# Two-layer diffusion trunk on one core: state tables, weight cuts and the context tail in another order

## The chip, the core and the metric

The kernel runs on one core of a Trainium2 chip. The metric is device time in microseconds (us), the median of several executions; lower is better. In what follows PE or TensorE is the matrix engine, DVE is VectorE, ACT is ScalarE, POOL is GpSimd, and SP is the engine that issues the DMAs named here. TensorE runs at one of two clock levels, 1.2 or 2.4 GHz; the profile gives the granted clock as a share of the higher one.

## The reference, cut to what matters

A latent stream `h` (1024 tokens by 1024) and a context stream `hc` (256 tokens) pass through two layers. Every layer is a mixer and a SwiGLU feed-forward, each behind a modulated RMSNorm and a gate. The context stream ends with layer 0's feed-forward; layer 1 uses its norm alone.

```python
for layer in range(2):
    sh1, sc1, g1, sh2, sc2, g2 = adaln(c, mod_w[layer], mod_b[layer])
    csh1, csc1, cg1, csh2, csc2, cg2 = adaln(c_ctx, mod_w[layer], mod_b[layer])
    n_lat = rms_norm(h, norm_g[layer, 0]) * (1 + sc1) + sh1
    n_ctx = rms_norm(hc, norm_g[layer, 0]) * (1 + csc1) + csh1
    if layer == 0:   # FNet groups + windowed attention, one input and one output projection
        o_lat, o_ctx = fourier_attention_mix(n_lat, n_ctx, mix_w_in, mix_w_out, ...)
    else:            # bidirectional diagonal state-space layer + GLU, context as its prefix
        o_lat, _ = s5_mix(n_lat, n_ctx, a_re, a_im, log_dt, b, c, d, glu_w)
    h = h + g1 * o_lat
    h = h + g2 * swiglu(rms_norm(h, norm_g[layer, 1]) * (1 + sc2) + sh2, w_gate, w_up, w_down)
    if layer == 0:
        hc = hc + cg1 * o_ctx
        hc = hc + cg2 * swiglu(rms_norm(hc, norm_g[layer, 1]) * (1 + csc2) + csh2, w_gate, w_up, w_down)
return rms_norm(h, final_g)
```

The state-space layer needs tables that depend on its parameters alone: for each pair of its 64 groups (32 "channels" here) a drive table, a readout table and a short kernel.

## The kernel before, in words

Each f32 matmul is three: both operands are split into a high half (a cast on ScalarE, `...h`) and a low half (a subtraction on VectorE, `...l`), and `mm3` (L155 to L157) multiplies high by high, low by high and high by low. A "cut" is the making of the two halves of a weight block (L1219, L1220); in layer 0's feed-forward the blocks of a weight pair are called A11, A12, A21 and A22, and S1 to S4 are sums of them, since the feed-forward on the latent rows goes by a Strassen scheme of seven products for eight.

The stretches on the time axis that the change touches:

- 175 to 300 us: the QKV projection, a loop over column blocks m in the order 4, 5, 0, 1, 2, 3, over three groups of tokens and over eight k steps (L942 to L970). The generator `tables(0, 12)` is stepped inside this loop, at k 2 and 5, and makes the tables of channels 0 to 11.
- 602 to 826: the context feed-forward, a loop over 22 units of 128 hidden columns (L1695 to L1733). Unit u cuts the weights of unit u+1 (`ccut`), runs its gate and up product (`cgate`, operand of the context `cx`), the down product of unit u-1 (`cdowns`) and the activation (`chidden`). In the middle of the gate `side()` steps `tables(12, 20)` and `prepare()`, which norms the latent rows for what follows.
- 826 to 845: the context tail (L1735 to L1753): gate, residual, sum of squares, norm, and eight stores to `udram`, from where the state-space layer reads the context.
- 826 to 1270: the steps `FA.step(s)` of the latent feed-forward, s from 0 to 10, with products pX, pY and pZ.
- 1270 to 1527: `FA.down`, the down projection on combined weights in raw slots (`rr`), with `tick0` once in 24 matmuls. It steps `behind2`, which holds `tables(20, 32, apart=True)` and `ssm_toeplitz` (whose last DMAs write `mtab`), and adds the residual of finished token tiles.
- 1527 to 1728: the state-space layer's front: `eload` brings drive tables (`El`) from DRAM, `pec` multiplies them with the context, ScalarE keeps the result (L1853), and the scan follows.

A table goes through `table_load` (its parameters by DMA, L576), `table_drive` (four copies on ScalarE, L584, and six products on GpSimd, L587 to L589, for one channel), `table_turn` (four transposes on TensorE, L596, a copy on ScalarE, L598, and a store to `etab`), `table_read` (four small matmuls, L608, a copy on ScalarE, L614, six products on VectorE, L619 to L621, and a store to `ftab`) and, for each second channel, `ssm_kt` (L628). The generator yields between these steps, and one call of it (`run(t, 1)`) goes as far as the next yield.

What sets the order: from the context feed-forward to the start of the scan SP, DVE, ACT and POOL issue in the order in which the code is written, one instruction behind the other, and an instruction that waits holds up all behind it on its engine. In the QKV loop only TensorE keeps the written order; a scheduler orders the others. `ctile()` gives one of six buffers in turn, raw slots (`wr0`, `wr1`, ...) are placed by name, and both are free again when their last reader is done.

## Time and profile before

| | us |
|---|---|
| median of 3 executions | 2667.91 (2664.15 to 2668.31) |
| profiled execution, device time | 2667.99 |
| profiled execution, span | 2666.2 |
| TensorE busy in the span | 2446.9 |
| VectorE busy | 1719.2 |
| ScalarE busy | 998.2 |
| GpSimd busy | 616.2 |

The mean granted clock of TensorE is 0.966. The span runs from the first to the last instruction of the profiled execution, and all positions on the time axis are counted from its start. A table of busy time tells which engine is loaded; where TensorE stands still is read from its list of waits, which names the line that waited, the engine and line that released it, and how long. From there the way leads to the releasing engine's timeline.

### The profile page before, as it was taken

How to read it: one execution, taken by the hardware profiler on the slowest of the kernel's cores; microseconds unless marked ns; L12 is line 12 of the kernel's file. 1: busy time of each engine (PE TensorE's matmuls, PEld its weight loads, DVE VectorE, ACT ScalarE, POOL GpSimd, SP SyncE). 2: the span in 40 equal slices, each digit the busy share in tenths (PEclk: the TensorE clock that was granted, in tenths of full speed). 3: DMA queues.
4: the chain of work that ended last, by engine and by line, in shares of the span. 5: the costliest groups of instructions: out<-in, count | busy, mean ns of one | idle time of the engine just before them, and what ended most of it. 6: DMA issues, size and time to landing. Idle time of an engine off the chain costs nothing.

```text
span 2666.2 us, 33521 instructions
## 1 busy us (share of the span) xinstructions
PE 2446.9 (92%) x12396; PEld 1967.4 (74%) x12396; DVE 1719.2 (64%) x2925; ACT 998.2 (37%) x1656; POOL 616.2 (23%) x867
## 2 busy tenths in 40 slices
PE   7999999997998999999899876499998999999996
PEld 4777677876897788888677654198876788887785
DVE  3648677675657766676577659932247676665556
ACT  4233466224554222222344482341253222223333
POOL 1235310122300122112444157511111112211000
PEclk9999999998999999999999987899999999999998
DMA  7642445535573544445766755624123545447653
GB/s 254 181 150 77 170 142 151 171 108 175 189 245 89 174 152 159 161 141 175 265 211 202 227 167 189 214 73 141 40 87 111 182 137 174 151 154 256 214 189 119
DMA packets 306900, 437.65 MB, mean 164 GB/s; under 512 B 71472, under 2 KB 176736, under 8 KB 306352
## 3 DMA queue, kind: packets, MB, share of 16 engines
q1 hardware_dynamic: 303600, 425.74, 48.0%
q0 software_dynamic: 3136, 9.77, 1.1%
q8 instruction: 98, 1.61, 0.2%
q14 instruction: 66, 0.54, 0.1%
HBM read 329.39 MB, written 111.17 MB: 165 GB/s over the span
## 4 chain that ended last, share of the span: by engine, by line
PE 65%; DVE 15%; ACT 5%; DMA 3%; issue 2%; SPq 0%; POOL 0%; DVEq 0%; ACTq 0%
PE pY L155 4%; PE pY L157 4%; PE pY L156 4%; PE pd L156 3%; PE pd L155 3%; PE pd L157 3%; PE pZ L157 3%; PE pZ L155 3%; PE pZ L156 3%; PE pX L157 3%; PE pX L155 3%; DVE SA L1990 3%; PE pX L156 3%; PE pft L2089 2%; PE pgl L155 2%
## 5 line engine op out<-in xcount | busy, mean ns | idle before, releaser
L1404 DVE TENSOR_TENSOR dl<-rr,dh 128x1024 fp32r<-128x1024 f32 x156 | 190.6, 1265 | 153.6 <-ACT dh L1403 153.6
L156 PE MATMUL pd<-dl,dh 128*128 128x512 f32 x616 | 244.6, 397 | 11.1 <-DVE dl L1404 11.1
L155 PE MATMUL pd<-dh 128*128 128x512 f32 x616 | 246.0, 399 | 7.2 <-DVE du L1425 2.4
L157 PE MATMUL pd<-dh,dl 128*128 128x512 f32 x616 | 242.9, 394 | 0.0
L1403 ACT CAST dh<-rr 128x1024 fp32r<-128x1024 f32 x156 | 153.8, 1034 | 194.5 <-PE pd L156 188.9
L1271 POOL TENSOR_TENSOR wd<-wd 128x512 f32<-128x512 f32 x22 | 32.2, 1464 | 810.6 <-DMA wd<-in_ffn_w_down 810.6
L1240 ACT ACTIVATE c<-c 128x512 f32<-128x512 f32 x66 | 41.8, 633 | 405.5 <-DVE c L1320 218.5
L156 PEld LDWEIGHTS pd<-dl,dh 128*128 128x128 f32 x616 | 117.4, 191 | 39.6 <-DVE dl L1404 16.0
L155 PEld LDWEIGHTS pd<-dh 128*128 128x128 f32 x616 | 117.4, 191 | 36.9 <-DVE du L1425 3.2
L157 PEld LDWEIGHTS pd<-dh,dl 128*128 128x128 f32 x616 | 117.3, 190 | 24.7
L155 PE MATMUL pgl<-wl_h,yTh 128*128 128x512 f32 x256 | 100.7, 393 | 0.0
L156 PE MATMUL pgl<-wl_l,yTh 128*128 128x512 f32 x256 | 100.1, 391 | 0.0
L1209 DVE TENSOR_TENSOR wr<-wr 128x1024 f32<-128x1024 f32 x65 | 99.1, 1525 | 1.4
L1990 DVE TENSOR_TENSOR SA<-SA,scan 128x48 f32<-128x48 f32 x508 | 91.1, 238 | 0.0
L2180 DVE TENSOR_TENSOR gsg<-gsg,pgl 128x256 f32<-128x256 f32 x32 | 13.4, 420 | 106.2 <-ACT gsg L2179 106.2
L1241 DVE TENSOR_TENSOR c<-c 128x512 f32<-128x512 f32 x66 | 47.6, 721 | 46.2 <-ACT c L1240 46.2
L227 PE MATMUL ada<-mw,cond 128*32 128x512 f32 x320 | 58.7, 622 | 18.8 <-DMA mw<-in_mod_w 18.7
L155 PE MATMUL pY<-xT2h,S2h 128*128 128x512 f32 x176 | 70.7, 402 | 4.7 <-ACT S2h L1219 4.7
L1990 POOL TENSOR_TENSOR SB<-SB,scan 128x32 f32<-128x32 f32 x254 | 69.7, 274 | 20.8 <-ACT SB L1914 1.0
L1240 ACT ACTIVATE c<-pX 128x512 f32<-128x512 f32 x21 | 12.6, 601 | 161.6 <-PE pX L157 161.6
L157 PE MATMUL pY<-xT2h,S2l 128*128 128x512 f32 x176 | 70.5, 400 | 2.6 <-DVE S2l L1220 2.6
L155 PE MATMUL pY<-xT3h,S3h 128*128 128x512 f32 x176 | 69.7, 396 | 3.1 <-DVE c L1298 3.1
(761 smaller groups left out, 7342.2 us busy)
## 6 DMA issues: line engine op xcount, KB each, us to landing
mw<-in_mod_w SPq DMA_DIRECT2D x96, 512.0 KB
rr<-hd SPq DMA_DIRECT2D x70, 512.0 KB
wr<-in_ffn_w_gate SPq DMA_DIRECT2D x66, 512.0 KB
wr<-in_ffn_w_up SPq DMA_DIRECT2D x66, 512.0 KB
hd<-c SPq DMA_DIRECT2D x66, 512.0 KB
wd<-in_ffn_w_down SPq DMA_DIRECT2D x22, 1024.0 KB
td<-wd SPq DMA_DIRECT2D x88, 256.0 KB
rr<-td SPq DMA_DIRECT2D x40, 512.0 KB
```

The lines of the kernel that those rows point to most:

```text
L155: nc.tensor.matmul(o, ah, bh, start=first, stop=False, **kw)
L156: nc.tensor.matmul(o, ah, bl, start=False, stop=False, **kw)
L157: return nc.tensor.matmul(o, al, bh, start=False, stop=last, **kw)
L227: nc.tensor.matmul(acc[32 * t:32 * t + 32, :], cond[:, k, :], w[:, q * 512:(q + 1) * 512], start=(k == 0 and not act), stop=(k == 7), tile ...
L1209: eng.tensor_sub(b(n), b(x), b(y))
L1240: nc.scalar.activation(c[:, 0], src[:, 0], AF.Silu)
L1241: nc.vector.tensor_mul(c[:, 1], c[:, 0], src[:, 1])
L1271: e.tensor_sub(b11, b12, b11)
L1403: nc.scalar.copy(hi[:, 0:m], t[:, a, 0:m])
L1404: nc.vector.tensor_sub(lo[:, 0:m], t[:, a, 0:m], hi[:, 0:m].bitcast(F32))
L1990: eng.tensor_add(cur, cur, tm[:, b])
L2089: nc.tensor.matmul(o_, T_[:, :, c_, g0], F_[:, g, c_, :], start=(n_ >= 2 and c_ == 0), stop=(c_ == 1 and (n_ >= 2 or g == 3)))
```

## The change

1. `tables()` yields between a table's load and its drive, and makes its further empty turn in each case but the `apart` one, where before it made it only with `slots`. The QKV loop calls the generator twice ahead of the loop and, in column block 3, at k 1, 4 and 6.
2. In the context feed-forward units 0 and 1 are both cut ahead of the loop, and the loop's first turn cuts nothing.
3. The context tail is taken apart: the gating stays, into two buffers `sc`; adds, squares and norm with the stores become hooks that step 0 of the latent feed-forward calls behind its first cuts, behind its A12 product, and ahead of its S1 cut. The stores write 16 values (64 bytes) in a run where they wrote 32 (128 bytes).
4. At the end of the down projection `eput(1)` loads the second pair of drive tables into the raw slot `wr0` as soon as a single raw block is left; `eload` follows for the third and fourth pair, and later ones move up in the same way. The `mtab` DMAs go out two in a turn.

```diff
@@ tables
         table_load(a // 2)
+        yield
         table_drive(a)
         yield
-        if slots:
+        if not apart:
             yield
@@ ssm_toeplitz
             nc.sync.dma_start(mtab[16 * jj:16 * jj + 16], ...)
-            yield
+            if jj % 2:
+                yield
@@ QKV
-    run(tq, 1)
+    run(tq, 2)
...
-                if k in (2, 5) and (m, gi) != (4, 0):
+                if k in ((1, 4, 6) if m == 3 else (2, 5)) and (m, gi) != (4, 0):
                     run(tq, 1)
@@ FA
+        def hook(self, n):
+            self.hooks.pop(n, lambda: None)()
@@ FA.step
                 self.cut(s, "A12")
                 if s == 0:
                     self.cutx("T3")
+            self.hook("T3")
...
                 self.cut(s, "S3")
                 self.close_step(s)
+                self.hook("A12")
                 self.first_hidden(s)
+                self.hook("c11")
             c11 = self.c.pop(s)[1]
             self.cut(s, "S1")
@@ context feed-forward
     ccut(0, 0)
     ccut(0, 1)
+    ccut(1, 0)
+    ccut(1, 1)
     cload(1)
...
-        if u + 1 < NHT:
+        if u + 1 >= NHT:
+            FA.cut(0, "A11")
+        elif u:
             ccut(u + 1, 0)
-        else:
-            FA.cut(0, "A11")
...
-        if u + 1 < NHT:
+        if u + 1 >= NHT:
+            wops[u] = wsplit1(cwd.pop(u))
+        elif u:
             ccut(u + 1, 1)
-        else:
-            wops[u] = wsplit1(cwd.pop(u))
@@ context tail
-    g2c = FA.ctile().rearrange("p a n -> p (a n)")
-    nc.sync.dma_start(g2c, row(0, 5, 1))
-    hc = [FA.ctile().rearrange("p a n -> p (a n)") for _ in range(2)]
+    hc, sc = ([FA.ctile().rearrange("p a n -> p (a n)") for _ in range(2)] for _ in range(2))
+    nc.sync.dma_start(sc[1], row(0, 5, 1))
     for t in range(2):
         nc.sync.dma_start(hc[t], hdram[8 + t])
     FA.load(1)
     cdowns(NHT - 1, wops.pop(NHT - 1))
     for t in range(2):
-        sc = wp.tile([P, D], F32, name="cgt", tag="ws", bufs=2)
-        nc.vector.tensor_mul(sc, cacc[t].rearrange("p a n -> p (a n)"), g2c)
-        nc.vector.tensor_add(hc[t], hc[t], sc)
-        nc.scalar.activation(sc, hc[t], AF.Square, accum_out=ssF[:, 10 + t:11 + t])
+        nc.vector.tensor_mul(sc[t], cacc[t].rearrange("p a n -> p (a n)"), sc[1])
+    def ctx_add():
+        for t in range(2):
+            nc.vector.tensor_add(sc[t], sc[t], hc[t])
+    def ctx_square():
+        for t in range(2):
+            nc.scalar.activation(hc[t], sc[t], AF.Square, accum_out=ssF[:, 10 + t:11 + t])
     def ctx_store():
         rs = rstd_finish(ssF[:, 10:12], "rC")
-        for q in range(2):
-            uc = FA.ctile()...
-            for i in range(2):
-                nc.vector.tensor_scalar_mul(uc[:, :, i, :], hc[i][:, 512 * q:512 * q + 512]..., rs[:, i:i + 1])
+        for t in range(2):
+            nc.scalar.mul(sc[t], sc[t], rs[:, t:t + 1])
             for a in range(4):
-                nc.sync.dma_start(udram[:, 32 * q:32 * q + 32, a, :], uc[a::4]...)
-    ctx_store()
+                nc.sync.dma_start(udram[:, :, a, 16 * t:16 * t + 16], sc[t][a::4].rearrange("p (g h) -> p g h", h=16))
+    FA.hooks = {"T3": ctx_add, "A12": ctx_square, "c11": ctx_store}
@@ down projection
+    def eput(n_, slots):
+        for ch, t in zip((2 * order8[n_], 2 * order8[n_] + 1), slots):
+            Et[ch] = t.rearrange("p (a b n) -> p a b n", a=4, b=2)
+            nc.sync.dma_start(Et[ch]..., etab[2 * ch:2 * ch + 2]...)
     def tick0():
         flush()
+        if not FA.queue and len(FA.rawq) == 1:
+            t = FA.place("wr0", "El", [P, 4, 512]).rearrange("p a n -> p (a n)")
+            eput(1, (t[:, 0:1024], t[:, 1024:2048]))
...
     FA.down(gained0, tick0)
-    run(bt)
     run(bh)
     flush()
     h = hf_
-    for n_ in range(1, 3):
+    for n_ in range(2, 4):
         eload(n_)
+    run(bt)
...
-        if n_ + 3 < 8:
+        if n_ < 2:
+            eload(n_ + 4)
+        elif 3 <= n_ < 5:
             eload(n_ + 3)
```

ScalarE at the start of the context feed-forward, before. A11h to A22h are the high halves of a unit's weight cuts, L584 is the drive of table 12, and `csg` and `chid` are a unit's activation.

```order
L1219 CAST A11h<-wr 128x1024
L1219 CAST A12h<-wr 128x1024
L1219 CAST A21h<-wr 128x1024
L1496 ACTIVATE nFscr,ssF_4929<-hb 128x1024
L584 COPY tE<-tpar 64x2x16 x4
L282 ACTIVATE nFrs<-nFrs 128x8
L1219 CAST A22h<-wr 128x1024
L1634 ACT_TABLE_LOAD
L1634 ACTIVATE csg<-gu 128x256
L1637 CAST chid<-csg 128x256
L137 CAST cw_h<-c 128x1024
L1219 CAST A11h<-wr 128x1024
```

ScalarE at the same place, after.

```order
L1224 CAST A11h<-wr 128x1024
L1224 CAST A12h<-wr 128x1024
L1224 CAST A21h<-wr 128x1024
L1224 CAST A22h<-wr 128x1024
L1504 ACTIVATE nFscr,ssF_4929<-hb 128x1024
L282 ACTIVATE nFrs<-nFrs 128x8
L1642 ACT_TABLE_LOAD
L1642 ACTIVATE csg<-gu 128x256
L1645 CAST chid<-csg 128x256
L137 CAST cw_h<-c 128x1024
L1224 CAST A11h<-wr 128x1024
L584 COPY tE<-tpar 64x2x16 x4
```

Both cuts of unit 1 now stand ahead of the table's copies, and these stand between the two cuts of unit 2.

ScalarE at the context tail, before. The rows from S2h on belong to step 0; L1739 is the square, L282 the root of the context's norm, and `xT3h`, `xT1h` are operands of the latent rows.

```order
L1219 CAST S2h<-wr 128x1024
L1739 ACTIVATE cgt,ssF_4929<-c 128x1024 x2
L282 ACT_TABLE_LOAD
L282 ACTIVATE rCrs<-rCrs 128x2
L1247 COPY c<-pX 128x1024
L1219 CAST A12h<-wr 128x1024
L1186 CAST xT3h<-rawB 128x1024 x2
L1219 CAST S3h<-wr 128x1024
L1240 ACT_TABLE_LOAD
L1240 ACTIVATE c<-pX 128x512
L1219 CAST S1h<-ws_7961 128x1024
L1186 CAST xT1h<-rawB 128x1024 x2
```

ScalarE at the same place, after. L1755 is the square, L1760 the scaling by the norm.

```order
L1224 CAST S2h<-wr 128x1024
L1252 COPY c<-pX 128x1024
L1224 CAST A12h<-wr 128x1024
L1191 CAST xT3h<-rawB 128x1024 x2
L1224 CAST S3h<-wr 128x1024
L1755 ACTIVATE c,ssF_4929<-c 128x1024 x2
L1245 ACTIVATE c<-pX 128x512
L282 ACT_TABLE_LOAD
L282 ACTIVATE rCrs<-rCrs 128x2
L1760 ACTIVATE c<-c,rCrs 128x1024 x2
L1224 CAST S1h<-ws_7961 128x1024
L1191 CAST xT1h<-rawB 128x1024 x2
```

The first cuts of step 0 follow S2h at once, and square, root and scaling stand between the cuts of S3 and S1.

SP's DMAs at the end of the down projection, before. `El` are drive tables, `hdram` takes the residual rows.

```order
L683 DMA mtab<-rdram 1024x1x128
L1806 DMA hdram<-hf 128x1024
L683 DMA mtab<-rdram 1024x1x128
L1806 DMA hdram<-hf 128x1024 x2
L683 DMA mtab<-rdram 1024x1x128
L1806 DMA hdram<-hf 128x1024 x4
L683 DMA mtab<-rdram 1024x1x128 x3
L1565 DMA El<-etab 128x2x512 x14
```

SP at the same place, after.

```order
L1399 DMA rr<-in_ffn_w_down 128x512
L684 DMA mtab<-rdram 1024x1x128 x2
L1826 DMA hdram<-hf 128x1024
L684 DMA mtab<-rdram 1024x1x128 x2
L1826 DMA hdram<-hf 128x1024 x2
L1799 DMA El<-etab 128x2x512 x2
L1826 DMA hdram<-hf 128x1024 x4
L1573 DMA El<-etab 128x2x512 x12
```

One pair of drive tables stands ahead of the last four residual stores, and no `mtab` DMA is left behind them.

## Rows read from the trace of the kernel before

**Rows 1.** the page, part 1: busy us, share of the span, instructions

```profile
PE 2446.9 (92%) x12396; PEld 1967.4 (74%) x12396; DVE 1719.2 (64%) x2925; ACT 998.2 (37%) x1656; POOL 616.2 (23%) x867
```

**Rows 2.** TensorE's waits, QKV projection, 180 to 300: total, times, longest us

```profile
PE pet L596 <- POOL tab L589: 4.5, 2, 2.7
PE psw L817 <- DVE ql L152: 3.6, 3, 2.9
```

**Rows 3.** TensorE's waits at the start of the context feed-forward, 600 to 640

```profile
PE gu L155 <- ACT A22h L1219: 12.6, 1, 12.6
PE gu L157 <- DVE A22l L1220: 4.4, 1, 4.4
```

**Rows 4.** timeline, TensorE, context tail: start, duration, operation [idle before <- releaser]

```profile
844.82 0.79 PE L155 MATMUL pX<-xB21h,A12h 128*128 128x512 f32 x1 [5.39 <-ACT A12h L1219]
...
853.05 0.40 PE L155 MATMUL pY<-xT3h,S3h 128*128 128x512 f32 x1
853.28 0.39 PE L156 MATMUL pY<-xT3l,S3h 128*128 128x512 f32 x1
...
859.44 0.50 PE L155 MATMUL pZ<-xT1h,S1h 128*128 128x512 f32 x1 [0.62 <-ACT xT1h L1186]
```

**Rows 5.** TensorE's waits at the start of the down projection, 1265 to 1300

```profile
PE pet L596 <- POOL tE L589: 9.3, 2, 6.2
```

**Rows 6.** timeline, TensorE, start of the state-space layer

```profile
1545.88 1.08 PE L1850 MATMUL pec<-El,UTc 128*32 128x256 f32 x8 [14.43 <-DMA El<-etab]
```

**Rows 7.** timeline, TensorE, gate of unit 2, across A11 and A12

```profile
637.45 0.28 PE L157 MATMUL gu<-cxh,A11l 128*128 128x256 f32 x1
637.57 0.28 PE L155 MATMUL gu<-cxh,A12h 128*128 128x256 f32 x1
```

**Rows 8.** timeline, GpSimd, drive of the first state table

```profile
188.49 0.90 POOL L589 TENSOR_TENSOR tab<-tab 128x256 f32<-128x256 f32 x1
```

**Rows 9.** slices of QKV: each engine's busy time, granted clock, DMA share, GB/s

```profile
190.00:195.00 5.00, 5.00 (x18) 4.20 (x17) 1.42 (x3) 1.17 (x2) 2.79 (x5) 0.53 0.14 52
255.00:260.00 5.00, 4.81 (x16) 3.85 (x17) 4.17 (x7) 0.12 (x1) 4.76 (x7) 0.66 0.01 3
```

**Rows 10.** timeline, VectorE, QKV projection

```profile
253.51 0.43 DVE L619 TENSOR_TENSOR tab<-tab 128x256 f32<-128x256 f32 x1 [1.63 <-DMA ftab<-tab]
```

**Rows 11.** timeline, ScalarE, start of the context feed-forward

```profile
620.08 0.90 ACT L584 COPY tE<-tpar 64x32 f32<-64x32 f32 x4 [12.51 <-DMA tpar<-par]
...
621.12 1.03 ACT L1219 CAST A22h<-wr 128x1024 fp32r<-128x1024 f32 x1
```

**Rows 12.** timeline, SP's DMA queue, the same place

```profile
611.36 2.25 SPq L576 DMA_DIRECT2D tpar<-par  x1
```

**Rows 13.** timeline, ScalarE, context tail

```profile
841.42 1.28 ACT L282 ACT_TABLE_LOAD   x1
...
843.72 1.05 ACT L1219 CAST A12h<-wr 128x1024 fp32r<-128x1024 f32 x1
```

**Rows 14.** timeline, SP's DMA queue, end of the down projection

```profile
1538.33 7.02 SPq L1565 DMA_DIRECT2D El<-etab  x8
```

**Rows 15.** slices at the end of down and in the state-space front

```profile
1520.00:1525.00 5.00, 5.00 (x23) 4.12 (x22) 2.78 (x9) 0.93 (x3) 0.00 (x0) 1.00 0.19 75
1550.00:1600.00 50.00, 44.67 (x653) 37.04 (x653) 29.71 (x91) 49.53 (x76) 33.84 (x97) 1.00 0.39 127
```

**Rows 16.** timeline, ScalarE, start of the state-space layer

```profile
1541.03 0.68 ACT L1979 COPY lam<-lam 128x64 f32<-128x64 f32 x4
1548.34 0.59 ACT L1853 COPY keep<-pec 128x512 f32<-128x512 f32 x1 [6.64 <-PE pec L1850]
```

**Rows 17.** slices of the context tail, behind the eight small stores

```profile
845.00:850.00 5.00, 4.96 (x11) 3.47 (x12) 5.00 (x5) 3.89 (x4) 0.00 (x0) 0.50 0.86 133
850.00:855.00 5.00, 5.00 (x23) 4.03 (x22) 1.44 (x3) 1.53 (x2) 0.00 (x0) 0.99 0.49 77
```

**Rows 18.** timeline, ScalarE, first reuse of the stores' buffers in step 1

```profile
885.54 1.01 ACT L1247 COPY c<-pX 128x1024 f32<-128x1024 f32 x1 [1.37 <-PE pX L157]
```

More of the change, by code (lines that the diff above doesn't have):

```diff
@@ L1150, in __init__ @@
             self.td = dr.tile([4, NP, P, 512], F32, name=f"td{l}")
-            self.b, self.op, self.x, self.c = {}, {}, {}, {}
+            self.b, self.op, self.x, self.c, self.hooks = {}, {}, {}, {}, {}
+        def hook(self, n):
+            self.hooks.pop(n, lambda: None)()
         def begin(self):
@@ L1735, in build_ @@
     for t in range(2):
-        sc = wp.tile([P, D], F32, name="cgt", tag="ws", bufs=2)
-        nc.vector.tensor_mul(sc, cacc[t].rearrange("p a n -> p (a n)"), g2c)
-        nc.vector.tensor_add(hc[t], hc[t], sc)
-        nc.scalar.activation(sc, hc[t], AF.Square, accum_out=ssF[:, 10 + t:11 + t])
+        nc.vector.tensor_mul(sc[t], cacc[t].rearrange("p a n -> p (a n)"), sc[1])
     pclose("ps")
     ps = popen("ps", None, space=PSUM)
+    def ctx_add():
[4 more added lines that the diff above has]
+            nc.scalar.activation(hc[t], sc[t], AF.Square, accum_out=ssF[:, 10 + t:11 + t])
     def ctx_store():
         rs = rstd_finish(ssF[:, 10:12], "rC")
-        for q in range(2):
-            uc = FA.ctile().rearrange("p a n -> p (a n)").rearrange("p (g i h) -> p g i h", g=32, i=2)
-            for i in range(2):
-                nc.vector.tensor_scalar_mul(uc[:, :, i, :], hc[i][:, 512 * q:512 * q + 512].rearrange("p (g h) -> p g h", h=16), rs[:, i:i + 1])
+        for t in range(2):
+            nc.scalar.mul(sc[t], sc[t], rs[:, t:t + 1])
             for a in range(4):
-                nc.sync.dma_start(udram[:, 32 * q:32 * q + 32, a, :], uc[a::4].rearrange("p g b h -> p g (b h)"))
-    ctx_store()
+                nc.sync.dma_start(udram[:, :, a, 16 * t:16 * t + 16], sc[t][a::4].rearrange("p (g h) -> p g h", h=16))
+    FA.hooks = {"T3": ctx_add, "A12": ctx_square, "c11": ctx_store}
     for s in range(NP):
@@ L1782, in build_ @@
     bh, bt = behind(), behind2()
+    def eput(n_, slots):
+        for ch, t in zip((2 * order8[n_], 2 * order8[n_] + 1), slots):
+            Et[ch] = t.rearrange("p (a b n) -> p a b n", a=4, b=2)
+            nc.sync.dma_start(Et[ch].rearrange("p (z a) b c -> p z (a b c)", z=2), etab[2 * ch:2 * ch + 2].rearrange("z p n -> p z n"))
     def tick0():
         flush()
+        if not FA.queue and len(FA.rawq) == 1:
+            t = FA.place("wr0", "El", [P, 4, 512]).rearrange("p a n -> p (a n)")
+            eput(1, (t[:, 0:1024], t[:, 1024:2048]))
         if loads0:
@@ L1807, in close @@
             if i == 4:
-                for e, ch in enumerate((2 * order8[0], 2 * order8[0] + 1)):
-                    Et[ch] = utc[e][:, 1024:2048].rearrange("p (a b n) -> p a b n", a=4, b=2)
-                    nc.sync.dma_start(Et[ch].rearrange("p (z a) b c -> p z (a b c)", z=2), etab[2 * ch:2 * ch + 2].rearrange("z p n -> p z n"))
+                eput(0, (utc[0][:, 1024:2048], utc[1][:, 1024:2048]))
         return [add, close] if q else [add]
     FA.down(gained0, tick0)
-    run(bt)
     run(bh)
```

## The prediction

> **What bounds the kernel now.** I read the page first: TensorE is busy for 2446.9 of 2666.2 us [rows 1], so what an edit can give is almost only time in which TensorE stands still or runs at its lower clock level. I then took the list of TensorE's waits for each stretch that the diff touches, looked up on the releasing engine what had kept it, and read the granted clock of the slices behind each wait. The reader is to see five places. In the QKV projection the tensor engine waits 4.5 us for the first state table and 2.9 us for a low half of a query tile [rows 2]. At the start of the context feed-forward it waits 12.6 and 4.4 us for one weight cut [rows 3]. At the context tail it waits 5.39 us for another cut [rows 4]. In the down projection it waits 9.3 us for the drive of table 20 [rows 5], and at the start of the state-space layer 14.43 us for tables from DRAM [rows 6]. Where I looked at the slices behind such waits, the matmuls ran at the lower level at first [rows 9, 17].
>
> **The change part by part.** The sum is made against the profiled execution, 2667.99 us, which is 0.08 us above the median of the runs, so no correction is needed.
>
> *QKV.* The empty turn of the table generator and the second call ahead of the loop put each table step one place later on TensorE; GpSimd's order stays. Between the old place of the first table's transposes and the new one lie six 512-wide matmuls, two of the rotation and nine 256-wide ones. A 512-wide step takes 853.28 - 853.05 = 0.23 us [rows 4], a 256-wide one 637.57 - 637.45 = 0.12 [rows 7], together 8 x 0.23 + 9 x 0.12 = 2.9 us. GpSimd finishes the second half of that table at 188.49 + 0.90 = 189.39, as before [rows 8]. TensorE now comes 2.9 us later, so the first wait (4.5 - 2.7 = 1.8) goes and the second becomes 2.7 + 1.8 - 2.9 = 1.6: gain 2.9. The following slice, 190 to 195, runs at 0.53 of the clock [rows 9], a loss of some 2.4 us; whether a 1.6 us wait still brings it is open, so 0 to 2.4 of it comes back, and I take 1. The 2.9 us wait of the rotation has a DVE cause: a table multiply (L619) waited 1.63 us for a DMA, ahead of the query tile's ops in DVE's queue [rows 10]. In the new order this multiply stands behind them, so the wait and the slice at 0.66 [rows 9], 1.5 us, can go: 0 to 4.4, I take 2.6. In the last column block three steps now go through each group where two did, and a new wait for GpSimd there could cost 1 to 2 us. QKV: **6.5** (2 to 8.3).
>
> *Context feed-forward.* TensorE stood at the cut A22 of unit 1, because ScalarE's queue had the copies of table 12 ahead of it, and these waited 12.51 us for their parameters' DMA, until 620.08; that DMA was issued at 611.36 behind four weight loads [rows 12]. A22's high half then came at 621.12 to 622.15 [rows 11], and TensorE waited 4.4 us more for its low half, which DVE makes behind four scalings of the residual rows [rows 3]. In the new order both halves of A22 stand ahead of these copies, and the weights are in SBUF, so both waits at this place go. The copies themselves still wait for the same DMA, which keeps its place on SP, and now A12 of unit 2 stands behind them: ScalarE is free at 620.08 + 0.90 = 620.98, casts A12 by 622.0, DVE subtracts by 623.2. With two matmuls of three needing only the high half, the product starts in effect at 622.9. TensorE is there earlier: from 609.6 (622.2 - 12.6) it has 36 gate matmuls of 0.12, 12 down matmuls of 0.23 and 12 gate matmuls, 8.5 us, or 618.1, later by a microsecond if the first down's split is late, which changes nothing. Before, that product began at 637.57 [rows 7]. Gain 637.57 - 622.9 = 14.7, less 0 to 2.5 because TensorE stands for about 4 us and what follows it may run at the lower level, as it did before behind its wait. Nothing is queued on ScalarE behind the waiting copies but this cut; the gates' activations of unit 1 wait in the same queue and cost no more than the cut does. I take **13.5** (12 to 15).
>
> *Context tail.* The norm of the context rows leaves the place between the S2 and the A12 product. There TensorE waited 5.39 us, since ScalarE squared twice, loaded a function table (1.28 us at 841.42) and cast A12 only at 843.72 [rows 13]; the product ran partly at half clock, in 8.23 us (844.82 to 853.05) [rows 4] instead of 24 x 0.23 = 5.5. With the cut right behind S2, A12 follows without a wait at 839.4 (844.82 - 5.39), and the S3 product starts at 839.4 + 5.5 = 844.9, which is 8.2 us early. Part of it is given back: the same square root, its table load and two 1024-wide scalings of about 1 us each now stand on ScalarE in front of the S1 cut and its operand (1.28 + 0.2 + 2 = 3.5 us), and the two adds and squares lie on DVE and ScalarE ahead of S3's end. The operand of S1 came 0.62 us late before, at 859.44 [rows 4]. In the new order I get 854.8 for it: 859.44 - 8.2 + 3.5. Gain 859.44 - 854.8 = 4.6, less 0 to 2.3 for slow matmuls behind a new wait of some 4.5 us. The gate row's load on SP now needs a buffer that comes free only when the last down weights are split, and the loads of the context rows and of step 1's weights queue behind it; these weights are read at the end of step 0, and the rows at the adds, so I cost it at 0 to 1. The Trainium skill (ScalarE: Activation LUTs, What ACT_TABLE_LOAD costs) gives a switch about 2.66 us, load and drain together. The trace disagrees: from the load's start to A12's cast are 2.30 us, with a square root and a 1 us copy between [rows 13]; by the page the gain would be 1.4 us smaller. I take **4** (2 to 5.5).
>
> *Down projection.* The drive moves behind the first tick's four casts on ScalarE, but the parameters' load and the transposes keep their places, and the 9.3 us of waits [rows 5] hang on that load and on GpSimd. I take **0.5** (0 to 1).
>
> *State-space start.* The second pair of tables was loaded behind the last four residual stores and three table DMAs, issued from 1538.33 [rows 14], and TensorE waited for it until 1545.88 [rows 6]. Now a freed raw slot takes it ahead of these stores; the DMA engines have room for it, at a share of 0.19 from 1520 to 1525 [rows 15], so it lands before the first pair's matmuls end. ScalarE then sets the pace: it finishes its previous work at 1541.71 and picked up the result at 1548.34 after 6.64 us idle [rows 16]. From 1550 to 1600 it is busy for 49.53 of 50 us [rows 15], so starting 6.6 us sooner passes through to the scan. The third pair's load moves up by the three table DMAs, 3 us, but is wanted 6.6 sooner: 0 to 1 lost. I take **6.5** (5.5 to 7).
>
> Sum: 6.5 + 13.5 + 4 + 0.5 + 6.5 = 31; 2668 - 31 = **2637**.
>
> **The rivals.** (1) *The context start hands its wait on.* Cutting unit 1 early fills ScalarE and DVE, the first down's split comes late, and behind the copies of table 12 the next cuts and activations pile up, so that unit 2 and 3 wait again. For it: DVE's backlog already made the low half of A22 come 4.4 us after the high one [rows 3], and the same DMA still holds ScalarE [rows 11]. Against: from 623 on every cut is a unit ahead. A second wait of 5 us and a slow stretch of 2.5 would leave 6 of 13.5: 2645. (2) *The early pair of tables does nothing*: its slot is freed only at the end of the down, or the pair queues behind the stores anyway. For it: the slot must be read by its last cast. Against: the load stands ahead of four stores in the new order. It would lose the 6.5: 2643.5. (3) *The down's wait goes too*, because the weights' casts ahead of the drive fill it, and the halves of the clock come back everywhere: another 9 us, 2628. Against: the load keeps its place. (4) *Slower than before: the small stores.* The context's 8 stores now write runs of 64 bytes, 2048 each, instead of 128 bytes, 1024 each. Before, they took 0.86 and 0.49 of all DMA engines for 5 us each [rows 17], 6.75 us. Their source buffers are written again in step 1, first by the copy of its first product, 885.54 [rows 18], some 34 us after the first store. At the same price for a run the stores take 13.5 us and are hidden. At 2.5 times that price the copy starts to wait for them; from 34 + 31 = 65 us on, about five times, they eat all the rest and the kernel is slower, 2673 at 70 us. The Trainium skill (DMA: Bandwidth & Descriptors, Specifications) states that writes under 512 bytes are done by read-modify-write, which speaks against this edit; the trace has 128-byte stores at 133 and 77 GB/s [rows 17], so the rule alone isn't a factor of five. No row shows a 64-byte store.
>
> **How the numbers follow.** Forecast, 2631 to 2642: 0.66. Rival 1: 0.14. Rival 2: 0.08. Rival 3: 0.05. A mixture of lost parts that ends within 0.2% (5 us, about what a measurement of this kernel can tell from no change): 0.05. Rival 4: 0.02. Adding the high ends of all terms gives 36.8, so 2631; with rival 3, 2628. The low ends give 21.5, so 2646.5, and rivals 1 or 2 with one further miss reach 2650. The range is 2626 to 2650. Faster 0.93, same 0.05, slower 0.02.
>
> **What would show it.** Right: no TensorE wait of over 3 us for A22 at 610 to 630 but one of about 4 for A12; none for A12 in the tail, and one of 4 to 5 for S1's operand; ScalarE's idle time ahead of the first copies behind the second pair under 1 us; the waits for table 20 still there. Wrong: a wait of 9 us or more at units 1 to 3; stores at the tail that last over 30 us; waits for GpSimd in the last column block of QKV.

## The result, and the profile after

The changed kernel takes 2638.59 us (median of four, 2637.16 to 2642.39) against 2668.11 us before; the ratio is 0.9895 with a 95% interval of 0.9882 to 0.9908, so 1.05% faster. The forecast was 2637. The total came out, but three of its five terms did not: QKV gave more, the context feed-forward and the state-space start gave less. These errors pull in opposite directions, so that the total came so near is in part luck.

The profiled execution of the changed kernel took 2642.39 us (span 2640.5), the slowest of its four. Since both profiles contain stretches that go differently from one execution to the next, the table also has a second profile of the kernel before (from the experiments below, span 2668.1). A stage's length is the difference of the starts of the named instructions in the timelines; `pft` stands here for the first readout product on the scan's result (`pft<-Ft,SB`), since other products of that name come earlier.

| stage, from one first instruction to the next | before | before again | after | gain against the mean of before | forecast |
|---|---|---|---|---|---|
| QKV and attention (`pqkv` to `pmo`) | 307.5 | 307.0 | 297.8 | 9.4 | 6.5 |
| context feed-forward (`gu` to `pX`) | 224.7 | 224.0 | 213.5 | 10.8 | 13.5 |
| context tail (`pX` to `pZ`) | 32.7 | 32.3 | 28.4 | 4.1 | 4 |
| latent steps (`pZ` to `pd`) | 409.0 | 409.9 | 410.7 | -1.3 | 0 |
| down (`pd` to `pec`) | 261.0 | 258.9 | 259.1 | 0.9 | 0.5 |
| state-space front (`pec` to VectorE's copy ahead of the scan) | 79.1 | 78.3 | 75.1 | 3.6 | 6.5 |
| scan (to `pft`) | 120.3 | 123.7 | 123.6 | -1.6 | 0 |
| all else | 1231.9 | 1234.0 | 1232.3 | 0.7 | 0 |

Now the lines of the changed kernel, stage by stage. TensorE's waits in QKV, 180 to 300 us (line, releaser, total, times, longest), answering [rows 2]:

```profile
PE pkt L628 <- ACT tab L614: 3.1, 2, 2.1
PE pet L596 <- POOL tab L589: 1.3, 1, 1.3
...
PE psw L819 <- DVE ql L152: 0.2, 1, 0.2
```

One wait of 1.3 us is left of the first table's 4.5, and the rotation's 2.9 is gone, as forecast. A new wait of 2.1 us stands at a later table step (`pkt`), where the wait for the same line summed to 1.2 us before; in the last column block, where the prediction feared a new wait for GpSimd, there is none. The slices behind the first table, answering the first row of [rows 9] (busy time of PE, PEld, DVE, ACT and POOL, granted clock, DMA share, GB/s):

```profile
185.00:190.00 5.00, 3.70 (x33) 3.16 (x31) 4.90 (x8) 1.18 (x2) 4.76 (x7) 1.00 0.14 52
190.00:195.00 5.00, 5.00 (x28) 4.20 (x25) 4.93 (x7) 4.61 (x12) 4.77 (x6) 1.00 0.21 74
```

In this execution the clock never leaves its higher level there (1.00, against 0.53 before). TensorE's waits at the start of the context feed-forward, 590 to 640, answering [rows 3]:

```profile
PE gu L155 <- ACT A12h L1224: 3.4, 1, 3.4
PE gu L157 <- DVE A12l L1225: 1.2, 1, 1.2
PE gu L157 <- DVE A11l L1225: 0.8, 1, 0.8
```

Both A22 waits are gone and one at A12 of unit 2 has come. ScalarE's timeline there, answering [rows 11] (start, duration, operation, idle before it and what ended it), and the slices behind the wait:

```profile
605.77 1.05 ACT L1224 CAST A11h<-wr 128x1024 fp32r<-128x1024 f32 x1 [3.42 <-DMA wr<-in_ffn_w_up]
610.97 0.90 ACT L584 COPY tE<-tpar 64x32 f32<-64x32 f32 x4 [4.15 <-DMA tpar<-par]
611.89 1.04 ACT L1224 CAST A12h<-wr 128x1024 fp32r<-128x1024 f32 x1
```

```profile
610.00:615.00 5.00, 0.84 (x3) 0.63 (x4) 2.71 (x4) 2.21 (x7) 3.96 (x5) 0.87 1.09 361
615.00:620.00 5.00, 5.00 (x25) 5.00 (x25) 3.71 (x3) 3.06 (x4) 4.84 (x6) 0.50 0.48 176
```

The drive's copies wait for the parameters and A12 stands behind them, as forecast; after it TensorE runs at half its clock for all of 615 to 620. At the context tail, TensorE's longest wait between 800 and 870, then ScalarE's timeline ahead of it, then the slices behind it (answering [rows 4], [rows 13], [rows 17]):

```profile
PE pZ L155 <- ACT xT1h L1191: 4.6, 1, 4.6
```

```profile
824.04 1.28 ACT L282 ACT_TABLE_LOAD   x1
825.34 0.20 ACT L282 ACTIVATE rCrs<-rCrs 128x2 f32<-128x2 f32 x1
825.77 2.19 ACT L1760 ACTIVATE c<-c,rCrs 128x1024 f32<-128x1024 f32 x2 [0.23 <-DVE rCrs L283]
827.87 1.03 ACT L1224 CAST S1h<-ws 128x1024 fp32r<-128x1024 f32 x1
```

```profile
825.00:830.00 5.00, 3.94 (x17) 2.82 (x15) 1.23 (x2) 3.66 (x5) 0.00 (x0) 1.00 0.33 39
830.00:835.00 5.00, 0.97 (x2) 0.47 (x3) 3.89 (x5) 2.53 (x3) 0.00 (x0) 0.71 1.60 94
835.00:840.00 5.00, 5.00 (x14) 3.94 (x15) 5.00 (x5) 3.58 (x4) 0.00 (x0) 0.60 1.78 84
```

The wait for A12 is gone and one for S1's operand is there. Behind the cut S1 in these rows VectorE makes its low half and then forms the operand `xT1`, so the delay of that cut goes through VectorE before ScalarE can cast the operand. The eight stores of 64-byte runs fill the last two slices. In the down projection the line of [rows 5] reads the same, to the tenth:

```profile
PE pet L596 <- POOL tE L589: 9.3, 2, 6.2
```

At the state-space start the second pair's product has no wait any more ([rows 6] has no counterpart). ScalarE's timeline, answering [rows 16]:

```profile
1514.88 0.68 ACT L1999 COPY lam<-lam 128x64 f32<-128x64 f32 x4
1515.46 0.57 ACT L1871 COPY keep<-pec 128x512 f32<-128x512 f32 x1
...
1523.10 0.58 ACT L1871 COPY keep<-pec 128x512 f32<-128x512 f32 x1
1526.76 0.46 ACT L1914 ACTIVATE UT<-put,shx,gsx 128x128 f32<-128x128 f32 x1 [3.08 <-DVE UT L1916]
```

The second `keep` follows at once, where 6.64 us were idle. But behind the third one ScalarE now idles for 3.08 us: the next operation in its queue is an input of the third group (`UT`), and this waits for VectorE, which is in the context tree (`Sc<-Sc,tct`). VectorE's last tree operation and its `UT`, then ScalarE at the same place in the kernel before:

```profile
1525.63 0.78 DVE L1902 TENSOR_TENSOR Sc<-Sc,tct 128x16 f32<-128x16 f32 x2
1526.33 0.72 DVE L1916 TENSOR_SCALAR UT<-put,gsx,shx 128x128 f32<-128x128 f32 x2
```

```profile
1556.65 0.59 ACT L1853 COPY keep<-pec 128x512 f32<-128x512 f32 x1
1557.12 3.79 ACT L1914 COPY SB<-pel 128x508 f32<-128x508 f32 x4
```

Before, the copies of a drive product (`SB<-pel`) stood there and ScalarE went on.

### The profile page after: what moved, and what is told of

It is laid out like the page before. It is cut to its first block, busy times and chain, and to the rows that moved or that the text cites. A ratio compares the mean times of both kernels' runs of the same rounds, so it can differ in the third digit from the quotient of the medians.

```text
span 2640.5 us, 33544 instructions
## 1 busy us (share of the span) xinstructions
PE 2450.1 (93%) x12396; PEld 1969.6 (75%) x12396; DVE 1716.0 (65%) x2921; ACT 999.3 (38%) x1658; POOL 613.6 (23%) x867
## 4 chain that ended last, share of the span: by engine, by line
PE 71%; DVE 16%; ACT 5%; DMA 4%; issue 3%; SPq 1%; POOL 1%; DVEq 0%; ACTq 0%
PE pY L157 4%; PE pY L155 4%; PE pY L156 4%; PE pd L156 3%; PE pd L155 3%; PE pd L157 3%; PE pZ L156 3%; PE pZ L157 3%; PE pZ L155 3%; PE pX L155 3%; PE pX L156 3%; PE pX L157 3%; DVE SA L2010 3%; PE pft L2109 2%; DVE scan L2006 2%
## 5 line engine op out<-in xcount | busy, mean ns | idle before, releaser
L2010 DVE TENSOR_TENSOR SA<-SA,scan 128x48 f32<-128x48 f32 x508 | 84.7, 225 | 0.0
L155 PE MATMUL pZ<-xT1h,S1h 128*128 128x512 f32 x176 | 69.7, 396 | 4.6 <-ACT xT1h L1191 4.6
```

The costliest lines, as they stand in the source:

```text
L155: nc.tensor.matmul(o, ah, bh, start=first, stop=False, **kw)
L2010: eng.tensor_add(cur, cur, tm[:, b])
```

## The experiments

**Each part alone.** Four kernels are the kernel before with one part of the change: QKV; the context feed-forward; the tail; the end of the down with the state-space start. The generator's yields, which all three of its users share, are made conditional, in the first as

```diff
         table_load(a // 2)
+        if not slots:
+            yield
         table_drive(a)
         yield
-        if slots:
+        if (not apart) if not slots else slots:
             yield
```

with `slots and not apart` and `apart` in the second and the fourth; the rest are the lines of the diff.

> The kernel before with the QKV part alone: in the QKV projection the table generator's load and drive are two steps, it makes an empty turn, is called twice ahead of the loop and three times in each group of column block 3; the other two uses of the generator are as before. Theory of the stage: TensorE's wait for the first table falls from 4.5 to about 1.3 us, the 2.9 us wait of the rotation goes, and with them both slices at the lower clock level; the context feed-forward then begins 8 to 10 us sooner and the time is 0.3 to 0.4% below before. Rival, by the sum on record: 6.5 us at this place and the rest of the 9.6 us seen there belongs to chance in the unchanged attention, so the gate of unit 0 begins 5 to 7 us sooner.

> The kernel before with the context feed-forward's part alone: units 0 and 1 both cut ahead of the loop, and the drive of table 12 a turn after its load. Theory: the 12.6 and 4.4 us waits go and one of 3 to 5 us for A12 of unit 2 comes, behind the copies that wait for the parameters' DMA; the matmuls behind it run at the lower level and cost 3 to 4 us, so the first product of step 0 begins 11 us sooner (10.5 to 12), not 13.5. Rival: the loss behind unit 2 came from the earlier start of the stage in the full change and doesn't show here, then it begins 13 to 15 us sooner.

> The kernel before with the context tail's part alone. Theory: no wait for A12, one of 4 to 5 us for the operand of S1, half of the stretch behind it at the lower level: step 1 begins 3 to 4 us sooner; the small stores take the DMA engines for 15 to 20 us and nobody waits for them. Rival: the tail's gain depends on the context part, then it is below 2 us or above 5.

> The kernel before with the parts at the end of the down projection and the state-space start alone (second pair of tables in a raw slot, two mtab DMAs in a turn, the drive a tick later). Theory: the first products of the second pair begin without a wait and the rotated inputs follow 8 to 11 us sooner, but the scan begins only 3 to 5 us sooner, since ScalarE's order in the front is another, and the scan itself takes 120 us or 124 us as its two engines happen to interlock: the time is 0 to 0.25% below before. Rival, by the sum on record: ScalarE passes the 6.6 us on to the scan and the time is 0.25% below before.

| part alone | ratio to before (95%) | its stage, us | stage of before, two profiles |
|---|---|---|---|
| QKV | 0.9956 (0.994 to 0.9973) | 298.4 | 307.5, 307.0 |
| context feed-forward | 0.9954 (0.994 to 0.9969) | 211.3 | 224.7, 224.0 |
| tail | 0.9987 (0.9978 to 0.9996) | 28.4 | 32.7, 32.3 |
| down's end and state-space start | 0.9984 (0.9975 to 0.9993) | 74.9 | 79.1, 78.3 |

The four reductions add up to 0.44 + 0.46 + 0.13 + 0.16 = 1.19%, against 1.05% for all together, within the intervals: no dependence between the parts shows. QKV kept 9 us, as its theory had it, though the first table's wait did not fall to 1.3 us. Its waits in QKV, 170 to 300, and the slice behind them:

```profile
PE pkt L628 <- ACT tab L614: 3.2, 2, 2.1
PE pet L596 <- POOL tab L589: 2.7, 1, 2.7
...
PE psw L819 <- DVE ql L152: 0.2, 1, 0.2
```

```profile
190.00:195.00 5.00, 5.00 (x26) 4.16 (x25) 4.90 (x7) 4.76 (x13) 4.76 (x7) 1.00 0.18 55
```

Here the first table cost 2.7 us in one wait and the clock still stayed up. That isn't a property of the kernel: in another profile with the same code in this stretch (the changed kernel of the section on the scan below) a single wait of the same length came ahead of a slow slice. Its waits from 180 to 200 and that slice:

```profile
PE pet L596 <- POOL tab L589: 2.7, 1, 2.7
```

```profile
190.00:195.00 5.00, 5.00 (x28) 4.12 (x28) 4.97 (x8) 3.84 (x8) 4.69 (x7) 0.66 0.14 52
```

Of the eight profiles that contain the QKV part, three have such a stretch in QKV, 3.4 us at the lower level; of the five that don't, four have two stretches of 6.8 and 3.4 us and one has the longer one alone.

The context part alone gave 224.3 (the mean of before) - 211.3 = 13.0 us, more than in the full change and more than its theory (10.5 to 12) allowed. The wait was there (2.9 and 0.8 us), so the rival in its own words did not hold either; but the stretch at the lower level behind it lasted 3.4 us here and 6.8 us in the changed kernel. In the six other profiles that contain the part unchanged that stretch is 3.4 or 6.8 us and the stage took 211.2 to 213.5, so the part gives 11 to 13. The tail alone took the same 28.4 us as in the full change, so its gain doesn't depend on the context part. The part at the state-space start brought TensorE's input transposes (`put`) 9.7 to 10.6 us nearer to `pec` (9.0 against 19.6 and 18.8), and the scan only 3.8 (78.7 - 74.9), both as its theory had it.

**What is left of the stall at unit 2.** On the changed kernel, the parameters of table 12 are loaded ahead of the weights of units 2 and 3.

```diff
     ccut(1, 1)
+    run(tb, 1)
     cload(1)
...
-    TBU = [1, 1, 1] + [2] * 13
+    TBU = [0, 1, 1] + [2] * 13
```

> The changed kernel, with the parameters of table 12 loaded ahead of the weights of units 2 and 3 on SP instead of behind them. Theory: what is left of the stall at unit 2 (3.4 and 1.2 us, and a slice at the lower clock level behind it) hangs on this DMA alone, so A12 follows A11 and the first product of step 0 begins 15 to 17 us after-to-before sooner counted from the gate of unit 0, against 11.2 in the changed kernel: 4 to 6 us less than the changed kernel. Rival: ScalarE is held by the weights of unit 2 themselves (A11 waited 3.42 us for its load), and the stall stays within 2 us of what it is.

The rival's number held: the stage took 213.1 us (213.5 in the changed kernel), the ratio to before is 0.9899 (0.9877 to 0.992). ScalarE's timeline:

```profile
603.14 1.04 ACT L1224 CAST A11h<-wr 128x1024 fp32r<-128x1024 f32 x1 [3.95 <-DMA wr<-in_ffn_w_up]
604.10 0.90 ACT L584 COPY tE<-tpar 64x32 f32<-64x32 f32 x4
606.99 1.04 ACT L1224 CAST A12h<-wr 128x1024 fp32r<-128x1024 f32 x1 [2.00 <-DMA wr<-in_ffn_w_up]
```

The copies no longer wait, but A12 waits 2.00 us for its own weights, and its cast begins 18.4 us behind the first gate where it began 20.2 us behind it. TensorE's wait for the high half falls from 3.4 to 0.7 us, but it then waits 2.4 us for the low half on VectorE, and runs at the lower level for 10.2 us instead of 6.8. Taking one wait away only showed the ones behind it: the transfers of unit 2, VectorE's subtraction, and the clock.

**The norm behind S1's cut.**

```diff
                 self.first_hidden(s)
-                self.hook("c11")
...
                 self.cutx("T1")
+            self.hook("c11")
             self.form(s, "S4")
```

> The changed kernel, with the norm and the stores of the context rows behind the cut S1 and its operand instead of ahead of them. Theory: the 4.6 us wait for the operand of S1 is the root, its table load and the two scalings on ScalarE; without them it falls below 1.5 us, the slices at 0.71 and 0.60 of the clock behind it go, and step 1 begins 4 to 7 us sooner than in the changed kernel. Rival: the operand is late by itself (VectorE forms it late), and the wait keeps over 3 us.

TensorE's waits for S1's operand, 795 to 835:

```profile
PE pZ L156 <- DVE xT1l L1192: 0.8, 1, 0.8
PE pZ L155 <- ACT xT1h L1191: 0.7, 1, 0.7
```

The wait of 4.6 us fell to 0.7 for the high half, with 0.8 for the low one, the tail from 28.4 to 24.4 us, and the slices from 820 to 835 ran at 1.00. Step 1 begins 3.2 us sooner (45.4 against 48.7 us behind the first `pX`), short of the 4 to 7 that the theory gave. Over all latent steps 1 us or more of the 3.9 came back (411.5 us; 409.3 to 410.7 in the kernels with the norm where the change puts it). The ratio to before is 0.9877 (0.9856 to 0.9897), which can't be told from the changed kernel's. So 3.9 of the 4.6 us were the root, its table load and the scalings, as the prediction had it.

**Table 20 two turns later.**

```diff
         table_load(a // 2)
         yield
+        if apart:
+            for _ in range(2):
+                yield
         table_drive(a)
```

> The changed kernel, with two more empty turns of the generator between load and drive of table 20 in the down projection, so that its transposes stand 48 matmuls later on TensorE. Theory: the 9.3 us of waits there hang on the load's 6.6 us and GpSimd's drive, which then lie beside the matmuls: the waits and the slow slices go, and the first products of the state-space layer begin 9 to 14 us sooner than in the changed kernel, counted from the first product of the down. Rival: the two turns come back at the end of the down, where the last tables and mtab DMAs are then late, and the scan begins less than 5 us sooner.

This is the largest gain of a single edit: 2624.77 us, ratio 0.9843 (0.9816 to 0.987). The waits for table 20 are gone and the slices there run at 1.00; the down takes 248.6 us instead of 259.1. Of these 10.5 us the state-space front gives 3.7 back (78.8 us; there ScalarE waits 6.7 us for VectorE instead of 3.1), so the rival has a part, though the scan still begins 6.8 us sooner, more than the 5 it allowed. The scan itself is 1.3 us shorter (122.3), and GpSimd, which starts its chain as early as in the changed kernel, is done with it 4.6 us earlier counted from VectorE's copy. Together that is 8.1 us; the medians differ by 13.8, and the rest lies in stretches whose code is the same, so it isn't shown to be this edit's. The change left this stall as it was: it moved the drive and kept the transposes' place.

**The context tree on GpSimd.**

```diff
-            ctx_tree(nc.vector, ScB, slice(0, 8), slice(NA, NA + 8))
-            ctx_tree(nc.gpsimd, ScB, slice(8, 16), slice(NA + 8, 64))
+            ctx_tree(nc.gpsimd, ScB, slice(0, 16), slice(NA, 64))
```

> The changed kernel, with the whole first context tree on GpSimd instead of half of it on VectorE. Theory: in the changed kernel ScalarE waits 3.1 us for VectorE's half of the third group's inputs, which stand behind this tree, and TensorE's drive products 3.0 us behind that; without the tree both go and the scan begins 2 to 4 us sooner, counted from the first products of the state-space layer, so that the full 6.6 us arrive. Rival: ScalarE is full for the rest of the front whatever its order, and the scan begins within 1 us of where it did; GpSimd's chain then starts some 8 us later and may end last.

The front took 72.4 us instead of 75.1: against 78.7 before, 6.3, which is the term of the prediction but for 0.2. ScalarE's timeline at the place where it had idled:

```profile
1522.22 0.58 ACT L1871 COPY keep<-pec 128x512 f32<-128x512 f32 x1
1522.68 0.47 ACT L1914 ACTIVATE UT<-put,shx,gsx 128x128 f32<-128x128 f32 x1
1523.54 1.04 ACT L1884 COPY Sc<-pex 64x512 f32<-64x512 f32 x1 [0.39 <-PE pex L1878]
```

The order on ScalarE is that of the changed kernel, and of the 3.08 us of waiting 0.39 us are left. From the start of the second `keep` to the end of the front ScalarE is idle for 1.0 of 60.3 us before, 3.6 of 63.0 in the changed kernel and 0.9 of 60.3 here: its work is the same 59.3 to 59.4 us, and the idle time is the whole difference. So the missing 2.7 us were the wait for VectorE's tree. GpSimd's chain starts 2.1 us later, not 8. The ratio to before is 0.9873 (0.9846 to 0.99); in the total this gain is not clear of the changed kernel's interval.

**The scan's two interleavings.** The kernel before once more, and the changed kernel with VectorE's copy ahead of the scan made three times:

```diff
-    nc.vector.tensor_copy(SA[:, 0], ScA[:, 31])
+    for _ in range(3):
+        nc.vector.tensor_copy(SA[:, 0], ScA[:, 31])
```

> The kernel before once more, to see which stage lengths of its first profile repeat. Theory that two interleavings of VectorE and GpSimd exist in the scan and an execution falls into one of them: the scan, 120.3 us in the first profile, takes 123 to 124 us as in the three kernels whose code there is that of before. Rival: the interleaving belongs to the kernel, then it takes 120 to 121 us again.

> The changed kernel, with VectorE's copy ahead of the scan made three times instead of once, so that its first product comes some 0.5 us later against GpSimd's chain. Theory of the interleaving: the phase at the start decides, a step then takes 1.085 us instead of 1.12 and the scan 119 to 121 us instead of 123.6, the time is 0.1% below the changed kernel. Rival: the slower interleaving draws the engines back from any start, and the scan takes 123 to 125 us.

The two costliest groups of VectorE from `pec` to `pft` (line, operation, shapes, count, busy us, mean ns), in the first profile of before, and then in its second one:

```profile
L1990 DVE TENSOR_TENSOR SA<-SA,scan 128x48 f32<-128x48 f32 x462 | 84.6, 242 | 0.0
L1986 DVE TENSOR_TENSOR scan<-SA,lam 128x96 f32<-128x96 f32 x232 | 53.7, 270 | 0.0
```

```profile
L1990 DVE TENSOR_TENSOR SA<-SA,scan 128x48 f32<-128x48 f32 x462 | 78.2, 227 | 0.0
L1986 DVE TENSOR_TENSOR scan<-SA,lam 128x96 f32<-128x96 f32 x232 | 63.4, 312 | 0.0
```

The same program, the same instructions, and in one execution the products take 270 ns, in another 312. VectorE's timeline in the middle of the scan shows the step, from one group of four sums to the next, in the first profile of before and then in the changed kernel:

```profile
1629.91 0.77 DVE L1990 TENSOR_TENSOR SA<-SA,scan 128x48 f32<-128x48 f32 x4
...
1630.99 0.77 DVE L1990 TENSOR_TENSOR SA<-SA,scan 128x48 f32<-128x48 f32 x4
```

```profile
1600.37 0.70 DVE L2010 TENSOR_TENSOR SA<-SA,scan 128x48 f32<-128x48 f32 x4
...
1601.49 0.70 DVE L2010 TENSOR_TENSOR SA<-SA,scan 128x48 f32<-128x48 f32 x4
```

A step of 1.08 us and one of 1.12. The scan of before again took 123.7 us, that of the changed kernel 123.6, so the 120.3 us against which the prediction was made belonged to that execution and not to the kernel. Delaying VectorE's start did not bring it back, as the rival had it (124.2 us; the median is 2639.8, the ratio 0.9904, 0.9891 to 0.9918), so what selects the faster interleaving stays open. The mean durations alone don't tell the two apart: in two more profiles (the QKV part alone and the early parameters) the products take 284 ns and the sums 240, and the step is 1.12 us all the same.

What the two engines cost each other shows at the end of the scan, where GpSimd has finished (at 1712.3 in the first profile) and VectorE goes on alone:

```profile
1714.80 0.57 DVE L1990 TENSOR_TENSOR SA<-SA,scan 128x48 f32<-128x48 f32 x4
1715.63 0.57 DVE L1990 TENSOR_TENSOR SA<-SA,scan 128x48 f32<-128x48 f32 x4
```

The same step now takes 0.83 us. Beside GpSimd's chain a step of VectorE is some 0.25 us longer in the faster interleaving and 0.3 us in the slower one.

**Three edits together** (norm behind S1, table 20 two turns later, the tree on GpSimd):

> The changed kernel with three of the edits together: the context's norm and stores behind the cut S1, two more empty turns ahead of the drive of table 20, the whole first context tree on GpSimd. Theory that they lie in stages of their own: their gains against the changed kernel add up, 2 + 13 + 3, to about 2620 us, 1.8% below before. Rival: in the state-space front the later tables of the down projection and the later start of GpSimd's chain meet, and 3 to 6 us of it are lost there, 2623 to 2627.

2618.1 us (2617.19 to 2623.08), ratio 0.9827 (0.9813 to 0.984), faster than both kernels. The sum of 2620 is met in the total. By stages it is less sure: from the tail to the scan the profile is 11 us shorter than the changed kernel's, and the rest of the 20.5 us between the medians lies in stretches whose code is the same. The front took 76.1 us (9.0 + 67.1), 3.7 more than with the tree alone, which is what the later table gave back by itself.

## Why the prediction was right, and where not

**The places were right.** Each of the five stalls did what the text said: one of the two waits for the first table went and 1.3 us stayed of the second (forecast 1.6; 1.3 to 2.7 in all eight profiles with this part); both A22 waits went and A12 of unit 2 took their place, 612.99 - 591.69 = 21.3 us behind the first gate (forecast 622.9 - 602.1 = 20.8); S1 came 28.4 us behind the first `pX` (forecast 854.8 - 826.76 = 28.0); table 20 kept its 9.3 us; ScalarE took up the second pair with no idle time. The tail gave 4.1 us where 4 were forecast, and the load of the function table took 1.28 us again with the root 0.02 us behind it, so a longer switch, which would have cost 1.4 us, did not show.

**QKV's term was mis-sized by its clock part.** The prediction took 1 of up to 2.4 us for the first slow slice and part of the second. Summed over the first 126 us from the first `pqkv`, in slices of 1 us, the busy time times what the clock lacked to 1 was 4.3 us before and 0.0 after, and TensorE's idle time fell from 9.8 to 5.2 us: 8.9 us, where the forecast was 6.5 with 8.3 as its end. This pair of executions is a fortunate one: over the five profiles without the part and the eight with it the two sums fall by 3.4 and 4.1 us, 7.5 together, inside the range. The whole stage up to `pmo` is 11.1 us shorter on average (307.2 to 296.1), and where the rest of that comes from, in the attention's unchanged code, isn't shown.

**The context's term was mis-sized the other way.** The wait came where it was forecast, but from A12 of unit 2 to the gate of unit 3 TensorE then needed 624.62 - 612.99 = 11.6 us, where 645.04 - 637.57 = 7.5 had been enough. Of these 4.2 us 1.2 are the wait for the low half and some 3 the slow matmuls; 1.1 came back by the stage's end. The price of "0 to 2.5" was too low for this execution, and the floor of 12 for this term was missed by 1.2 us (by nothing in the kernel with this part alone, 13.0). Over the five profiles without the part and the seven with it unchanged the gain is 12.0 us, at that floor.

**The step that failed** is "starting 6.6 us sooner passes through to the scan". It rested on a ScalarE busy for 49.53 of 50 us [rows 15], and, unsaid, on its queue staying as it was. The order in that stretch isn't written by hand: the part on the kernel lets the hand order reach to the scan, but it ends (`order.close()`) ahead of this front, and the scheduler put an input of the third group ahead of the drive's copies. 3.6 us of 6.5 arrived, as ScalarE stood idle for 3.08 us behind VectorE's context tree; with that tree out of the way 6.3 did.

**The baseline.** The scan of the profile that the sum was made against was 1.9 to 3.4 us shorter than in the eleven other profiles whose scan has the same code (122.2 to 123.7), and its layer-1 feed-forward (450.0 us from `pX` to `pd`) was at the low end of 450.0 to 453.4 in code that is the same in all. It stood at the median of the runs all the same, since other stretches were slow in it (the down 261.0 us, 258.9 in the second one). The changed kernel's profile has the long version of both and is the slowest of its four executions; it gains only 25.7 us in span while the medians differ by 29.5. That the first profile was a fair baseline in total is luck: its short scan and its long down projection cancel.

**The rivals.** The first (the wait handed on, 5 us and a slow stretch) came in a smaller form: 4.6 us, and 3 us of the term at most. The second (a useless early pair) and the third (the down's wait goes too) did not come; that the third would have been worth 9 us and more was borne out by moving the transposes. (The range's lower end was argued from 2628, which is the forecast less 9; all high ends with this rival would have been 2622.) The fourth, the small stores: the DMA engines' share is 1.60 and 1.78 from 830 to 840 and 0.33 ahead of it, together some 18 us, where 128-byte runs took 6.75. By this measure a run costs about 1.4 times as much as before, not 2.5. The share adds up the times of packets that overlap, which is how it can pass 1: from the first packet to the last the stores took 11.6 us, against 7.4 before. Nobody waits for them. The Trainium skill's rule on writes under 512 bytes (DMA: Bandwidth & Descriptors, Specifications) bears on the runs of both kernels, so it could not tell them apart; no run here shows whether it is at work.

## What to carry to other kernels

Cost a removed stall together with the slow matmuls behind it, which can be worth as much again (4.3 us beside 4.6 of waits in QKV between the two profiles), and read them from several executions, since the clock behind the same wait differs from one to the next. Where an order is left to a scheduler, compare the queue of the engine that is to pass the gain on, not only of the one that waited. Profile the baseline twice: a stretch in which two engines interlock can differ by 3% between executions of the same program.

## What the runs showed of the hardware

Waits of TensorE of 1.8 and 2.7 us within 3.2 us of each other (before) were followed by a slice at 0.53 of the clock, and 3.4 and 1.2 us (context) by 0.50. A single wait of 2.7 us was followed by full clock in one profile (QKV part alone) and by a slice at 0.66 in another with the same code there, so the length of one wait did not decide it. In the scan VectorE and GpSimd settle into one of at least two interleavings: in the faster one a step takes 1.08 us (products 270 ns, sums 242 ns), in the slower one 1.12 us (312 and 227 ns, or 284 and 240); without GpSimd beside it the step takes 0.83 us. Eight stores of 64-byte runs added up 2.7 times the packet time of eight of 128-byte runs with the same bytes, and took 1.6 times as long from first packet to last.
